# A decoder trunk on one core: other places in SBUF for the tiles

## The chip, the core and the metric

The kernel runs on one core of one Trainium2 chip. The time is device microseconds of that core, as the median of several executions; lower is better. Names used below: PE is TensorE's matmul, PEld its weight load, DVE is VectorE, ACT is ScalarE, POOL is GpSimd, SP is SyncE, whose queue issues nearly all DMAs. SBUF is the on-chip memory, 128 partitions; a tile here has all 128 partitions and a number of bytes in each. "Place" means the byte within the partition at which a tile starts, and "phase" that place modulo a power of two.

## The reference

The reference is a decoder trunk of two layers over 256 tokens of width 2048, in float32. Layer 0 is a recurrent block, layer 1 a sliding-window attention block; each is followed by a SwiGLU FFN of width 5632. Between the layers one K/V is projected.

```python
def swiglu_ffn(x, g, w_in, w_out):
    h = rms_norm(x, g)
    gate, up = jnp.split(h @ w_in, 2, axis=-1)
    return x + (jax.nn.silu(gate) * up) @ w_out

def recurrent_block(x, g, w_in, conv_w, conv_b, w_rg, b_rg, w_ig, b_ig, lam, w_out):
    h = rms_norm(x, g)
    y_branch, x_branch = jnp.split(h @ w_in, 2, axis=-1)
    xb = causal_depthwise_conv(x_branch, conv_w, conv_b)
    hs = rg_lru(xb, w_rg, b_rg, w_ig, b_ig, lam)
    return x + (hs * jax.nn.gelu(y_branch)) @ w_out

def reference(...):
    for layer in range(DEPTH):        # DEPTH = 2, N_REC = 1
        if layer < N_REC:
            x = recurrent_block(x, ...)
        else:
            if layer == N_REC:
                k_band, v_band = shared_kv(x, kv_norm_g, w_kv, k_norm_g)
            x = attn_block(x, ..., k_band, v_band)
        x = swiglu_ffn(x, norm2_g[layer], ffn_w_in[layer], ffn_w_out[layer])
    return x
```

## The kernel before

The activations are held transposed: features in the partitions, the 256 tokens along the free axis. The residual stream is four tiles x0 to x3 of 4 x 256 float32.

All weights are read once, as a stream of tiles of 128 x 1024 float32 (512 KB; 256 rows by 512 columns of a weight matrix). `stream` (line 271) runs over them. For job i it issues the load of tile i+4 on SP's queue (`load`, line 228, into raw[i % 4]), splits tile i+3 (`split`, line 254) and emits the matmuls of tile i. To split means to write each float32 number as the sum of two that the matmul type float32r holds: ScalarE copies raw to hi (line 259), and VectorE writes lo = raw - hi (line 260). The activations are split in the same way into slots of 2 x 256 columns (`split_act`, line 405; `gained`, line 411): the first 256 columns hold the high part, the second 256 the low part. A product then takes three matmuls of 256 moving columns on line 323: weights hi by activation high, hi by low, lo by high. Where two PSUM banks are at hand, the first two are one matmul of 512 columns ("h" in `PARTS`, line 287); `products` (line 289) does this in runs of three. In these the stationary operand is a slice of 128 columns (512 bytes) of hi or lo, and the moving operand is a slot (1024 or 2048 bytes). In the K/V projection (lines 841 to 843) it is the other way round for the values: a slice of hi or lo moves.

The other work (norms, convolution, recurrence, softmax, the activation functions) is cut into small tasks that `run_bg` (line 200) puts between the matmuls, by a count of the time that VectorE and ScalarE are behind. The order of all instructions is fixed when the program is built.

The tiles are made in the constructor (lines 70 to 97) and in `run` (lines 1039 to 1043). Each pool places its tiles one behind the other in the order in which they are made, each rounded up to 32 bytes; the 58 slots get their places when each is first used. The order before is: par, con and cc (parameters and constants), x0 to x3, raw0 to raw3, hi0 to hi3, lo0 to lo3, then the scratch tiles t0 to t3 and h0 to h7 of 256 float32, rstd0 and rstd1 (the per-token scale, 258 float32), acc, sq0 and sq1, then the slots s0 to s57 of 2048 bytes, and in a second pool nm, nt, r2 and rr0 to rr3.

Of the kernel before, what the change touches and what calls it, by code (L numbers as in the profile page):

```python
# [12 lines left out]
F32 = mybir.dt.float32  # L13
F32R = mybir.dt.float32r
# [3 lines left out]
P = 128  # L18
D = 2048
T = 256  # L20
# [20 lines left out]
class Val:  # L41


    def __init__(self, ap=None):
        self.ap = ap
        self.ready = False


class Trunk:
# [18 lines left out]
    def __init__(self, ctx, tc, dram):  # L68
        self.tc, self.nc, self.d = tc, tc.nc, dram
        nc = self.nc  # L70
        const = ctx.enter_context(tc.tile_pool(name="const", bufs=1))
        psum = ctx.enter_context(tc.tile_pool(name="psum", bufs=1, space=bass.MemoryType.PSUM))
        tmp = ctx.enter_context(tc.tile_pool(name="tmp", bufs=1))
        self.tmp = tmp
        self.par = const.tile([P, NPAR], F32, name="par")
        self.con = const.tile([P, NCON], F32, name="con")
        self.cc = const.tile([P, 32], F32, name="cc")
        self.x = [const.tile([P, 4, T], F32, name=f"x{i}") for i in range(4)]
        self.slots = deque(range(58))
        self.spool = const  # L80
        self.held = {}
        self.raw = [const.tile([P, 1024], F32, name=f"raw{i}") for i in range(4)]
        self.hi = [const.tile([P, 1024], F32R, name=f"hi{i}") for i in range(4)]
        self.lo = [const.tile([P, 1024], F32R, name=f"lo{i}") for i in range(4)]
        self.banks = deque(psum.tile([P, 512], F32, name=f"b{i}") for i in range(8))
        self.misc = 0
        self.started = False
        self.xin = 0
        self.other = None
        self.runs = 0  # L90
        self.since = 0
        self.hold = False
        self.tmps = deque(const.tile([P, T], F32, name=f"t{i}") for i in range(4))
        self.halves = deque(const.tile([P, T], F32, name=f"h{i}") for i in range(8))
        self.rstd = [const.tile([P, T + 2], F32, name=f"rstd{i}") for i in range(2)]
        self.acc = const.tile([P, T], F32, name="acc")
        self.sq = deque(const.tile([P, T], F32, name=f"sq{i}") for i in range(2))
        self.jobs = []
        self.bg = deque()
        self.tick = -2 * self.LD  # L100
        self.dve = 0.0
        self.act = 0.0
# [186 lines left out]
    def products(self, todo, st, hi, lo, x2, last, keep=False, paired=False):  # L289
# [7 lines left out]
        while rest:  # L297
            if not ticked and n >= half and not (self.since == 0 and rest[0][2] == "h"):
                self.half_tick()
                ticked = True  # L300
            if self.other is not None:
                self.runs = self.RUNS
            if not keep and self.runs and rest[0][2] != "h":
                left = set(rest)
                run = [(k, f) for k in range(2) for f in range(4) if ps[f][1] and (k, f, "a") in left
                       and (k, f, "b") in left][:3]
                new = ps[rest[0][1]][1] and ps[rest[0][1]][2] not in begun
                due = self.other is not None or self.since % 3 == 1 and self.since > 3
                if len(run) == 3 and (new or due and ps[run[0][1]][2] in begun):
                    self.runs -= 1  # L310
                    rest = [(k, f, "h") for k, f in run] + [q for q in rest if q[:2] not in run or q[2] == "l"]
            k, f, p = rest.pop(0)
            n += 1 + (p == "h")
            self.since = 0 if p == "h" else self.since + 1
            high, c0, c1 = self.PARTS[p]
            w = (hi if high else lo)[:, k * 512 + f * P:k * 512 + f * P + P]
            args = (ps[f][0][:, 0:c1 - c0], w, x2[k][:, c0:c1])
            kw = dict(start=ps[f][2] not in begun, stop=last and all(q[1] != f for q in rest), skip_group_check=paired)
            if self.other is not None and p == "h":
                with self.tc.issue_after(self.other):  # L320
                    self.nc.tensor.matmul(*args, **kw)  # L321
            else:
                self.nc.tensor.matmul(*args, **kw)  # L323
            self.other = None
            begun.add(ps[f][2])
# [710 lines left out]

    def run(self):
        nc, d = self.nc, self.d
        const = self.tmp
        self.nm = const.tile([P, T + 2], F32, name="nm")  # L1040
        self.nt = const.tile([P, T + 2], F32, name="nt")
        self.r2 = const.tile([P, 2], F32, name="r2")
        self.rrs = [const.tile([P, 48], F32, name=f"rr{i}") for i in range(4)]
        self.rv = {i: Val() for i in range(4)}
        self.rstd = {0: self.rstd[0], 1: self.rstd[1], 2: self.rstd[0], 3: self.rstd[1]}
        vals = lambda: [Val() for _ in range(ND)]
        self.xs0, x1, xk, x2, x3 = (vals() for _ in range(5))

        def first():
            for k in range(ND):  # L1050
                while k >= self.xin:
                    yield 1
                self.gained(k, [(C_N1A, self.xs0)])
                yield 2 * (k == 1)
            for k in range(ND):
                yield from self.squares(k)
            yield from self.norm(0, self.NORM0)
            self.decay()
        self.spawn(first())

        self.lru([(C_N2A, x1)], 1)
        self.ffn(0, x1, 1, [(C_KVG, xk)], 2)
        self.kv(xk, 2, [(C_N1B, x2)])
        self.attn(x2, 2, [(C_N2B, x3)], 3)
        self.ffn(1, x3, 3, None, None, out=d["out"])
        self.stream()
# [64 lines left out]
```

## Time and profile before

| What | us |
|---|---|
| median of 3 runs | 1990.03 (1989.65 to 1990.34) |
| span of the profiled execution | 1988.6 |
| PE, first and last matmul of line 268 | start 1.2 to 4.3 |
| DVE busy | 1271.2 |
| ACT busy | 1067.9 |

The span runs from the first to the last instruction of the profiled execution; it is 1.4 us below the median of the runs.

How the views are read: the page's busy line gives, for each engine, the time with at least one instruction in flight. Matmuls are pipelined, so a matmul's duration (its latency) overlaps the next one's; the distance between two starts in the timeline is what a matmul costs in a stream. The timeline joins neighbouring instructions of one group into a row with the first one's start, the row's length and a count; a weight load (PEld) stands beside the matmul before it. The chain that ended last is followed back from the last instruction to whatever released each one.

### The profile page before, as it was taken

Reading aid. Unit: us, or ns where it says so; the run is one execution under the profiler, and the core shown is the slowest. Engines: PE = TensorE matmul, PEld = TensorE weight load, DVE = VectorE, ACT = ScalarE, POOL = GpSimd, SP = SyncE. Lnnn points to the kernel's source line nnn. Section 1 sums busy time; section 2 is a strip of 40 time slices with the busy share of each in tenths; the row PEclk is TensorE's granted clock in tenths of the full one; section 3 lists DMA queues with packets and bytes.
Section 4 is the critical chain, followed back from the end, with each engine's and each line's share of the span. In section 5 each row is a group of like instructions: output and inputs, shape, how many; then the busy total and the mean of one; then the engine's idle time right before and its main releaser. Section 6 shows DMA issues by size and latency. Waiting matters only on the chain.

```text
span 1988.6 us, 40066 instructions
## 1 busy us (share of the span) xinstructions
PE 1982.0 (100%) x16684; PEld 1935.5 (97%) x16684; DVE 1271.2 (64%) x2049; ACT 1067.9 (54%) x1624; POOL 0.2 (0%) x4
## 2 busy tenths in 40 slices
PE   9999999999999999999999999999999999999999
PEld 9999999999999999999999889999999999999999
DVE  8988876556556655545668786755565565554453
ACT  7798655444444444444556775544454454444442
POOL 0000000000000000000000000000000000000000
PEclk9999999999999999999999999999999999999999
DMA  8555655565556555556555435565566656656663
GB/s 279 185 187 182 211 191 192 196 196 191 192 195 196 191 192 196 195 191 194 197 186 167 134 101 163 188 197 195 191 193 196 195 191 194 197 193 203 204 208 128
DMA packets 105302, 376.58 MB, mean 189 GB/s; under 512 B 11808, under 2 KB 14240, under 8 KB 105120
## 3 DMA queue, kind: packets, MB, share of 16 engines
q1 hardware_dynamic: 104832, 373.88, 57.8%
q8 instruction: 130, 2.13, 0.4%
q14 instruction: 52, 0.43, 0.1%
q10 hardware_dynamic: 288, 0.14, 0.0%
HBM read 371.88 MB, written 2.10 MB: 188 GB/s over the span
## 4 chain that ended last, share of the span: by engine, by line
PE 99%; ACT 0%; DVE 0%; DMA 0%; issue 0%; ACTq 0%
PE b L323 94%; PE b L334 2%; PE b L641 1%; PE b L331 1%; PE b L832 1%; ACT s L113 0%; PE b L321 0%; PE b L841 0%; PE b L842 0%; PE b L843 0%; DMA x<-in_x 0%; DVE s L131 0%; DVE lo L260 0%; ACT L113 0%; DVE s L122 0%
## 5 line engine op out<-in xcount | busy, mean ns | idle before, releaser
L323 PE MATMUL b<-s,hi 128*128 128x256 f32 (+1 forms) x10276 | 1431.9, 285 | 0.4 <-ACT s L113 0.4
L323 PEld LDWEIGHTS b<-s,hi 128*128 128x128 f32 x10276 | 1313.4, 188 | 30.4 <-ACT s L113 0.7
L260 DVE TENSOR_TENSOR lo<-raw,hi 128x1024 fp32r<-128x1024 f32 (+1 forms) x705 | 861.4, 1223 | 651.2 <-ACT hi L259 648.1
L259 ACT ACTIVATE hi<-raw 128x1024 fp32r<-128x1024 f32 (+1 forms) x705 | 745.7, 1059 | 817.7 <-PE b L323 756.7
L323 PE MATMUL b<-s,lo 128*128 128x256 f32 x5504 | 831.8, 277 | 0.0
L323 PEld LDWEIGHTS b<-s,lo 128*128 128x128 f32 x5504 | 720.4, 188 | 2.4 <-issue 0.8
L113 ACT ACTIVATE s<-h 128x256 fp32r<-128x256 f32 (+1 forms) x106 | 40.8, 411 | 23.8 <-DVE h L122 23.8
L113 ACT ACTIVATE t<-b 128x256 f32<-128x256 f32 x136 | 49.8, 374 | 2.5 <-PE b L323 0.3
L113 ACT ACTIVATE s<-x,par 128x256 fp32r<-128x256 f32 x80 | 38.6, 499 | 19.3 <-DVE x L122 13.6
L113 ACT ACTIVATE s<-s 128x256 f32<-128x256 f32 (+1 forms) x112 | 39.6, 409 | 5.7 <-DVE s L126 5.5
L113 ACT ACTIVATE h<-h 128x256 f32<-128x256 f32 (+1 forms) x104 | 38.8, 375 | 2.1
L113 ACT ACT_TABLE_LOAD x30 | 38.5, 1283 | 0.5
L126 DVE SCALAR_TENSOR_TENSOR s<-x,par,s 128x256 fp32r<-128x256 f32 x80 | 37.5, 482 | 1.4 <-ACT s L113 0.8
L122 DVE TENSOR_TENSOR h<-b,rstd 128x256 f32<-128x256 f32 x100 | 37.6, 417 | 0.0
L122 DVE TENSOR_TENSOR x<-x,b 128x256 f32<-128x256 f32 x64 | 24.1, 418 | 21.0 <-PE b L323 21.0
L113 ACT ACTIVATE s<-s,h 128x128 f32<-128x128 f32 x64 | 28.3, 443 | 13.3 <-DVE h L131 13.2
L122 DVE TENSOR_TENSOR h<-h,rstd 128x256 f32<-128x256 f32 x94 | 35.4, 419 | 0.0
L122 DVE TENSOR_TENSOR h<-h,h 128x256 f32<-128x256 f32 x88 | 35.0, 420 | 0.4 <-ACT h L113 0.4
L122 DVE TENSOR_TENSOR s<-h,s 128x256 fp32r<-128x256 f32 x88 | 35.2, 420 | 0.1
L122 DVE TENSOR_TENSOR h<-b,t 128x256 f32<-128x256 f32 x92 | 34.6, 417 | 0.0
L122 DVE TENSOR_TENSOR s<-s,s 128x256 fp32r<-128x256 f32 (+1 forms) x80 | 30.9, 422 | 3.5 <-ACT s L113 3.5
L334 PE MATMUL b<-s,s 64*128 64x256 f32 (+3 forms) x292 | 29.0, 302 | 0.1
(99 smaller groups left out, 566.4 us busy)
## 6 DMA issues: line engine op xcount, KB each, us to landing
raw<-in_ffn_in SPq DMA_DIRECT2D x352, 512.0 KB, 3.5
raw<-in_ffn_out SPq DMA_DIRECT2D x176, 512.0 KB, 4.3
raw<-in_lru_in SPq DMA_DIRECT2D x63, 512.0 KB, 3.6
raw<-in_lru_out SPq DMA_DIRECT2D x32, 512.0 KB, 3.7
raw<-in_w_q SPq DMA_DIRECT2D x32, 512.0 KB, 3.3
raw<-in_w_o SPq DMA_DIRECT2D x32, 512.0 KB, 3.3
raw<-in_gate SPq DMA_DIRECT2D x8, 512.0 KB, 3.9
raw<-in_kv SPq DMA_DIRECT2D x8, 512.0 KB, 4.3
```

Of the source, the lines that this page charges most:

```text
L113: self.nc.scalar.activation(out, in_, func, **kw)
L122: self.nc.vector.tensor_tensor(out, a, b, op)
L126: self.nc.vector.scalar_tensor_tensor(out, a, s, b, op0, op1)
L259: self.nc.scalar.activation(hi[:, q], raw[:, q], AF.Copy)
L260: self.nc.vector.tensor_tensor(lo[:, q], raw[:, q], hi[:, q].bitcast(F32), ALU.subtract)
L323: self.nc.tensor.matmul(*args, **kw)
L331: self.other = self.ins(f(*args, **kw))
L334: self.other = self.ins(f(*args, **kw))
L641: nc.tensor.matmul(out[j], (hi if high else lo)[:, c:c + P], x2[kt][:, q:q + T], start=kt == 0 and high > q, stop=kt == 1 and not high)
L832: nc.tensor.matmul(ps[f][:, 0:T], w0, x2[kt][:, q:q + T], start=k0 + kt == 0 and high > q, stop=k0 + kt == ND - 1 and not high)
```

## The change

The change only alters the order in which tiles are made, and adds one tile that nothing uses. After par, con and cc come the small tiles (rstd0, rstd1, nm, nt, r2, rr0 to rr3), then a tile `gap` of 160 float32 (640 bytes), then the scratch tiles t, h, acc and sq, then x, raw, hi and lo; the slots follow as before. The second pool is gone: nm, nt, r2 and rr come from the first.

```diff
-        tmp = ctx.enter_context(tc.tile_pool(name="tmp", bufs=1))
-        self.tmp = tmp
         self.par = const.tile([P, NPAR], F32, name="par")
         self.con = const.tile([P, NCON], F32, name="con")
         self.cc = const.tile([P, 32], F32, name="cc")
+        self.rstd = [const.tile([P, T + 2], F32, name=f"rstd{i}") for i in range(2)]
+        self.nm = const.tile([P, T + 2], F32, name="nm")
+        self.nt = const.tile([P, T + 2], F32, name="nt")
+        self.r2 = const.tile([P, 2], F32, name="r2")
+        self.rrs = [const.tile([P, 48], F32, name=f"rr{i}") for i in range(4)]
+        self.gap = const.tile([P, 160], F32, name="gap")
+        self.tmps = deque(const.tile([P, T], F32, name=f"t{i}") for i in range(4))
+        self.halves = deque(const.tile([P, T], F32, name=f"h{i}") for i in range(8))
+        self.acc = const.tile([P, T], F32, name="acc")
+        self.sq = deque(const.tile([P, T], F32, name=f"sq{i}") for i in range(2))
         self.x = [const.tile([P, 4, T], F32, name=f"x{i}") for i in range(4)]
+        self.raw = [const.tile([P, 1024], F32, name=f"raw{i}") for i in range(4)]
+        self.hi = [const.tile([P, 1024], F32R, name=f"hi{i}") for i in range(4)]
+        self.lo = [const.tile([P, 1024], F32R, name=f"lo{i}") for i in range(4)]
         self.slots = deque(range(58))
...
-        self.raw = [const.tile([P, 1024], F32, name=f"raw{i}") for i in range(4)]
-        self.hi = [const.tile([P, 1024], F32R, name=f"hi{i}") for i in range(4)]
-        self.lo = [const.tile([P, 1024], F32R, name=f"lo{i}") for i in range(4)]
...
     def run(self):
         nc, d = self.nc, self.d
-        const = self.tmp
-        self.nm = const.tile([P, T + 2], F32, name="nm")
...
```

The places that follow, as the built programs have them (bytes within the partition, and the same modulo 2048):

| Tiles | before | after |
|---|---|---|
| x0 | 21984 (1504) | 43008 (0) |
| raw0, hi0, lo0 | 38368, 54752, 71136 (1504 each) | 59392, 75776, 92160 (0 each) |
| t0, t1 | 87520, 88544 (1504, 480) | 27648, 28672 (1024, 0) |
| acc, sq0 | 101920, 102944 (1568, 544) | 39936, 40960 (1024, 0) |
| slots, s0 | 104992 (544) | 108544 (0) |
| rstd0, rstd1 | 99808, 100864 (1504, 512) | 21984, 23040 (1504, 512) |
| par, con | 16512, 17632 (128, 1248) | the same |

More of the change, by code (lines that the diff above doesn't have):

```diff
@@ L92, in __init__ @@
         self.hold = False
[L93 to L97, printed above, removed]
         self.jobs = []
@@ L1038, in run @@
         nc, d = self.nc, self.d
-        const = self.tmp
-        self.nm = const.tile([P, T + 2], F32, name="nm")
-        self.nt = const.tile([P, T + 2], F32, name="nt")
-        self.r2 = const.tile([P, 2], F32, name="r2")
-        self.rrs = [const.tile([P, 48], F32, name=f"rr{i}") for i in range(4)]
         self.rv = {i: Val() for i in range(4)}
```

## Prediction

> **What bounds the kernel now.** I read the page first, then the groups by form, then the timeline of TensorE and of its weight loads. The reader should see in the page that TensorE is never out of work, at the full granted clock, and that the chain that ended last is TensorE alone.
>
> ```profile
> span 1988.6 us, 40066 instructions
> PE 1982.0 (100%) x16684; PEld 1935.5 (97%) x16684; DVE 1271.2 (64%) x2049; ACT 1067.9 (54%) x1624; POOL 0.2 (0%) x4
> PEclk9999999999999999999999999999999999999999
> PE 99%; ACT 0%; DVE 0%; DMA 0%; issue 0%; ACTq 0%
> ```
>
> So only two things can move the end: the spacing of the matmuls, or a new wait in front of TensorE. The groups by form say which matmuls there are (count, then busy us and mean ns of one; the mean is a latency, not a spacing):
>
> ```profile
> L323 PE MATMUL b<-s,hi 128*128 128x256 f32 x9570 | 1291.3, 277 | 0.4 <-ACT s L113 0.4
> L323 PE MATMUL b<-s,lo 128*128 128x256 f32 x5504 | 831.8, 277 | 0.0
> L323 PE MATMUL b<-s,hi 128*128 128x512 f32 x706 | 201.6, 393 | 0.0
> ```
>
> That is 9570 + 5504 = 15,074 matmuls of 256 columns and 706 of 512 on line 323. The spacing is read from starts in the timeline (start us, busy us, engine, group, count):
>
> ```profile
> 1976.12 0.98 PEld L323 LDWEIGHTS b<-s,lo 128*128 128x128 f32 x8
> 1976.23 1.07 PE L323 MATMUL b<-s,lo 128*128 128x256 f32 x8
> ...
> 1977.13 1.98 PE L323 MATMUL b<-s,hi 128*128 128x256 f32 x16
> ...
> 1978.95 1.07 PE L323 MATMUL b<-s,lo 128*128 128x256 f32 x8
> ...
> 1979.85 1.98 PE L323 MATMUL b<-s,hi 128*128 128x256 f32 x16
> ...
> 1981.67 1.07 PE L323 MATMUL b<-s,lo 128*128 128x256 f32 x8
> ...
> 1982.57 0.39 PE L323 MATMUL b<-s,hi 128*128 128x256 f32 x2
> ```
>
> From 1976.23 to 1982.57 there are 8+16+8+16+8 = 56 matmuls in 6.34 us, 113.2 ns each. The load of the first one's weights starts at 1976.12, 110 ns ahead of it, so almost the whole spacing is one weight load. Loads with nearly no matmul behind them (the moving operand has one column) come at 42.20, 42.31, 42.42 and 42.53, 0.33 us for three, 110 ns each:
>
> ```profile
> 42.20 0.30 PEld L334 LDWEIGHTS b<-con,acc 128*128 128x128 f32 x2
> 42.31 0.30 PEld L334 LDWEIGHTS b<-con,acc 128*128 128x128 f32 x2
> 42.42 0.19 PEld L334 LDWEIGHTS b<-con,acc 128*128 128x128 f32 x1
> 42.53 0.19 PEld L321 LDWEIGHTS b<-s,hi 128*128 128x128 f32 x1
> ```
>
> A 256-column matmul is therefore paced by its weight load. A 512-column one is not: in a run of three the starts lie 0.23 us apart.
>
> ```profile
> 1223.37 0.62 PE L323 MATMUL b<-s,hi 128*128 128x512 f32 x2
> 1223.60 0.62 PE L323 MATMUL b<-s,hi 128*128 128x512 f32 x2
> 1223.83 0.62 PE L323 MATMUL b<-s,hi 128*128 128x512 f32 x3
> ```
>
> There is a second spacing for 256 columns. Here 8+16+8 matmuls, from 157.69 to 161.46, take 3.77 us, 117.8 ns each:
>
> ```profile
> 157.69 1.10 PE L323 MATMUL b<-s,lo 128*128 128x256 f32 x8
> 158.64 2.05 PE L323 MATMUL b<-s,hi 128*128 128x256 f32 x16
> 160.52 1.10 PE L323 MATMUL b<-s,lo 128*128 128x256 f32 x8
> 161.46 2.05 PE L323 MATMUL b<-s,hi 128*128 128x256 f32 x16
> ```
>
> **The change part by part.** It removes no instruction and adds none. In the two built programs the five engines have the same instructions in the same order with the same waits, and SP's queue has the same DMA issues; nothing is moved past a queue. What moves is the place of the tiles inside a partition. Before, x, raw, hi and lo start 1504 bytes past a multiple of 2048, the split activations 544 past it, t and h alternately at 1504 and 480. Every one of these lies 32 past a multiple of 64. After, x (43008 = 21 x 2048), raw, hi, lo and the split activations start at multiples of 2048, the scratch tiles at multiples of 1024. The gap tile is never read or written. So each access has to be priced by kind.
>
> *256-column matmuls and their weight loads.* Does their spacing know the address? All starts on line 323 share the remainder 32 by 64, so the trace has no aligned case. It has other phases, however. On lines 841 to 843 the moving operand is a slice of the weights (480 past 2048) and the stationary one an activation; on line 832 it is the other way round (moving at 544 or 1568):
>
> ```profile
> 1018.46 0.28 PE L842 MATMUL b<-lo,s 128*128 128x256 f32 x1
> ...
> 1019.37 0.39 PE L832 MATMUL b<-s,hi 128*128 128x256 f32 x2
> ...
> 1020.73 0.28 PE L841 MATMUL b<-hi,s 128*128 128x256 f32 x1
> ...
> 1021.91 0.28 PE L842 MATMUL b<-lo,s 128*128 128x256 f32 x1
> ```
>
> Eight matmuls up to 1019.37 take 0.91 us, 114 ns each; the twelve of line 832 up to 1020.73 take 1.36 us, 113 ns each; and ten more up to 1021.91 take 1.18 us, 118 ns each. Both spacings occur with the same phases, and the fast one occurs with either. I take 0 for this term. Its bounds: down to the 110 ns of a load alone, 15,074 x 3.2 ns = 48 us less (an estimate); up to 117.8 ns throughout, 15,074 x 4.6 ns = 69 us more (an estimate, a little high, since some run so already).
>
> *512-column matmuls.* [...] Lower bound: two spacings of a load alone, 220 ns, so 706 x 10 ns = 7 us less. Upper bound: two of the slow spacing, 236 ns, 4 us more. I take 0, as the activations' halves at 544 and 1568 serve the same spacing.
>
> [...]
>
> *VectorE and ScalarE.* The per-token scale has two tiles: rstd0 starts 32 past a multiple of 64, rstd1 on one. Most of the first group below are the FFNs' and read rstd1; the second is the recurrent block's and reads rstd0 (min/median/max ns):
>
> ```profile
> L122 DVE TENSOR_TENSOR h<-h,rstd x94: 416/419/433, 154.9 to 1746.6; 128x256 f32<-128x256 f32 x94
> L122 DVE TENSOR_TENSOR s<-s,rstd x8: 417/420/426, 50.5 to 76.2; 128x256 f32<-128x256 f32 x8
> ```
>
> 419 against 420 ns: the operand's place does not show. A gain here would be worth nothing, since TensorE waits for neither engine. A loss would be covered by their idle time, except where VectorE is nearly full:
>
> ```profile
> 0.00:20.00 20.00, 18.41 (x110) 17.39 (x111) 13.74 (x38) 15.21 (x28) 0.20 (x4) 1.00 0.89 328
> 20.00:160.00 140.00, 140.00 (x1193) 138.27 (x1192) 129.34 (x252) 111.58 (x188) 0.00 (x0) 1.00 0.62 199
> ```
>
> (Columns: window, length, busy us and count of PE, PEld, DVE, ACT, POOL, granted clock, DMA share, GB/s.) VectorE is busy for 129.34 of 140 us there, so a VectorE 8% slower would fill that stage; 10% would cost 142.3 - 140 = 2 us. I take 0.
>
> *DMA.* The share is 0.62 there. A load lands 3.5 us after its issue, and the split that uses it (line 259) waits for TensorE to free its hi tile, not for a DMA:
>
> ```profile
> L259 ACT ACTIVATE hi<-raw 128x1024 fp32r<-128x1024 f32 x703 | 744.5, 1060 | 816.8 <-PE b L323 756.7 <-issue 41.9 <-PE b L843 5.9
> raw<-in_ffn_in SPq DMA_DIRECT2D x352, 512.0 KB, 3.5
> ```
>
> So faster or slower writes stay hidden behind 756.7 us of such waits. Only the start is exposed, in the chain of waits:
>
> ```profile
> 1.16 3.34 DMA x<-in_x
> 5.16 36.78 PE b L323 x274
> ```
>
> The first projection matmul at 5.16 us stands behind a 3.34 us transfer. A tenth of that is 0.3 us either way, the bound of this term; I take 0.
>
> **Sum.** 0 + 0 + 0 + 0 on the profiled span of 1988.6 us. The runs' median is 1990.03 us, 1.4 us above the span, and that is the same for both programs. Forecast: 1990.0 us, no change.
>
> **The rivals.**
>
> *Faster: the two reads of TensorE cost less at aligned places.* For it: 113.2 ns is above the 110 ns of a load alone, and 230 ns is above twice that, while TensorE waits for nothing, so something in the operand supply costs 3 ns in 256 columns and 10 ns in 512. All starts share one remainder by 64, so alignment can be that something. Against it: the loads alone have the same remainder and need only 110 ns, and other phases change nothing. If only the 512s gain, 1990.0 - 7 = 1983 us. With half of the rest, 1990.0 - 7 - 24 = 1959 us; with all of it, 1990.0 - 55 = 1935 us. [...]
>
> *Slower: the slow spacing spreads.* Before, the weights' start and the moving operand's start differ by 1504 - 544 = 960 bytes, 448 by 512; after, by 0, so both of TensorE's reads begin at the same phase. If such reads get in each other's way, the state with 117.8 ns is entered more often. For it: that state exists, lasts over whole stages and shows no other engine as its cause. Against it: it occurs at both phases of the rows from 1018 to 1022. A quarter of the 256s costs 15,074 x 4.6 / 4 = 17 us, so 2007 us; all of them 69 us, 2059 us. It decides from 4 us on, some 900 matmuls.
>
> *The change does not do what it says.* A tile placed elsewhere by the allocator would leave the old remainders. The built program has the addresses given above, so this holds only for effects: it is the forecast.
>
> **How the numbers follow.** About 0.2%, 4 us, is what a measurement of this kernel can tell from no change. No change 0.42, its own range 1986 to 1994. Faster 0.33: 0.12 for the 512s alone near 1983, 0.12 for up to half of the rest, 0.09 beyond that. Slower 0.25: 0.16 for up to a quarter and a bit, 0.09 beyond. Together 8 in 10 need 1958 to 2018, which leaves out the 0.09 and 0.09 at the ends. The predicted time is that of the likeliest case.
>
> **What would show it.** Right: the spacing in the last 56 matmuls stays 113 ns, runs of 512 columns stay at 230 ns, the stretch from 157 to 161 us still shows 118, and the split of line 259 keeps its mean of 1060 ns. The faster rival shows as a 256 spacing near 110, or a 512 spacing near 220, everywhere at once. The slower one shows as 118 in stretches that have 113 now. A first projection matmul well away from 5.16 us would make the DMA term wrong; a wait of TensorE for VectorE between 20 and 160 us would make the cover wrong.

## The result, and the profile after

| | before | after |
|---|---|---|
| median of 4 runs, us | 1990.12 (1989.65 to 1990.34) | 2086.48 (2086.18 to 2086.78) |
| profiled span, us | 1988.6 | 2084.4 |

The changed kernel is slower: the ratio is 1.0484, with a 95% interval of 1.0471 to 1.0497. The spans differ by 95.8 us. Lines of the changed file stand three further down: 323 is now 326, 259 is 262.

The page of the kernel after, in the lines that answer to those shown of before:

```profile
span 2084.4 us, 40066 instructions
PE 2076.7 (100%) x16684; PEld 2029.1 (97%) x16684; DVE 1272.6 (61%) x2049; ACT 1065.3 (51%) x1624; POOL 0.2 (0%) x4
...
PEclk9999999999999999999999999999999999999999
...
PE 99%; ACT 0%; DMA 0%; DVE 0%; SPq 0%; issue 0%
```

The instruction counts are the same, the granted clock is the same, and TensorE is as fully in use as before. VectorE and ScalarE are busy for as long as before. TensorE is idle for 2084.4 - 2076.7 = 7.7 us, where it was idle for 6.6. So it has no new wait that counts; each matmul takes more time. The timeline near the end of the kernel after (start us, busy us, engine, group, count):

```profile
2072.48 2.08 PE L326 MATMUL b<-s,hi 128*128 128x256 f32 x16
2074.40 1.12 PE L326 MATMUL b<-s,lo 128*128 128x256 f32 x8
2075.36 2.08 PE L326 MATMUL b<-s,hi 128*128 128x256 f32 x16
2077.28 1.12 PE L326 MATMUL b<-s,lo 128*128 128x256 f32 x8
2078.24 0.40 PE L326 MATMUL b<-s,hi 128*128 128x256 f32 x2
```

From 2072.48 to 2078.24 there are 48 matmuls in 5.76 us, 120.0 ns each, where there were 113.2. This is not a feature of the end. The windows of a long, even stretch of both kernels say the same; the columns are the window, its length, busy us and count for PE, PEld, DVE, ACT and POOL, the clock, the DMA share and GB/s. Before:

```profile
400.00:1000.00 600.00, 600.00 (x5104) 592.26 (x5103) 348.93 (x454) 284.53 (x370) 0.00 (x0) 1.00 0.60 194
```

After:

```profile
400.00:1000.00 600.00, 600.00 (x4831) 591.82 (x4830) 326.06 (x424) 263.27 (x342) 0.00 (x0) 1.00 0.56 184
```

In 600 us TensorE gets through 4831 matmuls instead of 5104, 5.3% fewer, with a busy row that looks the same. The count, not the busy time, shows the loss. Everything else only follows: fewer matmuls, so fewer splits and fewer loads.

The other terms of the prediction, in the groups and the timeline of after. The weight loads with nearly no matmul behind them:

```profile
43.41 0.30 PEld L337 LDWEIGHTS b<-con,acc 128*128 128x128 f32 x2
43.51 0.30 PEld L337 LDWEIGHTS b<-con,acc 128*128 128x128 f32 x2
43.63 0.19 PEld L337 LDWEIGHTS b<-con,acc 128*128 128x128 f32 x1
43.74 0.19 PEld L324 LDWEIGHTS b<-s,hi 128*128 128x128 f32 x1
```

Three of them still take 0.33 us, 110 ns each. A load alone has not become slower. The runs of 512 columns:

```profile
1323.93 0.63 PE L326 MATMUL b<-s,hi 128*128 128x512 f32 x2
1324.16 0.62 PE L326 MATMUL b<-s,hi 128*128 128x512 f32 x2
1324.40 0.51 PE L326 MATMUL b<-s,hi 128*128 128x512 f32 x2
```

They start 0.23 to 0.24 us apart, hardly more than before. The split, VectorE's products with the two scale tiles (min/median/max ns), and the first matmuls of the projection:

```profile
L262 ACT ACTIVATE hi<-raw 128x1024 fp32r<-128x1024 f32 x703 | 743.2, 1058 | 923.7 <-PE b L326 839.8 <-issue 50.9 <-ACT h L116 18.2
```

```profile
L125 DVE TENSOR_TENSOR h<-h,rstd x94: 406/415/420, 159.3 to 1828.5; 128x256 f32<-128x256 f32 x94
L125 DVE TENSOR_TENSOR s<-s,rstd x8: 412/416/426, 51.8 to 77.8; 128x256 f32<-128x256 f32 x8
```

```profile
5.26 1.49 PE L326 MATMUL b<-s,hi 128*128 128x256 f32 x6 [0.68 <-ACT s L116]
```

The split takes 1058 ns where it took 1060, the products 4 ns less, and the first matmul comes 0.1 us later. None of this carries 96 us.

A finer number is used below, "the mean spacing": over the trace's starts of all 256-column matmuls of the projections' line (15,015 to 15,038 of them in each run), the mean distance to the next matmul's start, gaps outside 100 to 130 ns left out. It is 113.6 ns before and 119.8 after. Then 15,074 x 6.2 ns = 93 us, and the 706 of 512 columns went from 229.5 to 232.5 ns (in the same way, gaps outside 200 to 260 ns left out), 706 x 3.0 = 2 us. Together 95 us of the 95.8.

### The profile page after: what moved, and what is told of

Its sections match the earlier page's. It is cut to its first block, busy times and chain, and to the rows that moved or that the text cites. A ratio compares the mean times of both kernels' runs of the same rounds, so it can differ in the third digit from the quotient of the medians.

```text
span 2084.4 us, 40066 instructions
## 1 busy us (share of the span) xinstructions
PE 2076.7 (100%) x16684; PEld 2029.1 (97%) x16684; DVE 1272.6 (61%) x2049; ACT 1065.3 (51%) x1624; POOL 0.2 (0%) x4
## 4 chain that ended last, share of the span: by engine, by line
PE 99%; ACT 0%; DMA 0%; DVE 0%; SPq 0%; issue 0%
PE b L326 94%; PE b L337 2%; PE b L644 1%; PE b L334 1%; PE b L835 1%; DMA raw<-in_lru_in 0%; ACT s L116 0%; PE b L324 0%; PE b L845 0%; PE b L844 0%; PE b L846 0%; DVE s L134 0%; ACT L116 0%; DVE lo L263 0%; ACT hi L262 0%
## 5 line engine op out<-in xcount | busy, mean ns | idle before, releaser
L326 PE MATMUL b<-s,hi 128*128 128x256 f32 (+1 forms) x10276 | 1495.0, 291 | 1.7 <-ACT hi L262 1.0
L326 PEld LDWEIGHTS b<-s,hi 128*128 128x128 f32 x10276 | 1368.8, 191 | 33.1 <-ACT hi L262 1.4
L262 ACT ACTIVATE hi<-raw 128x1024 fp32r<-128x1024 f32 (+1 forms) x705 | 744.5, 1057 | 926.0 <-PE b L326 839.8
L326 PE MATMUL b<-s,lo 128*128 128x256 f32 x5504 | 865.3, 283 | 0.0
L326 PEld LDWEIGHTS b<-s,lo 128*128 128x128 f32 x5504 | 751.0, 192 | 2.3 <-issue 0.8
L116 ACT ACTIVATE h<-h 128x256 f32<-128x256 f32 (+1 forms) x104 | 34.3, 370 | 0.0
```

What stands on the lines that cost most here:

```text
L116: self.nc.scalar.activation(out, in_, func, **kw)
L262: self.nc.scalar.activation(hi[:, q], raw[:, q], AF.Copy)
```

## The experiments

Each was executed once, beside the kernel before on the same chip, which took 1989.4 to 1990.4 us there. In the theories, "distance" is the start of the activations' slots minus the start of hi and lo, modulo 256; slices are multiples of 512 bytes and halves of 1024, so one number holds for all matmuls of the projections. Before it is 544 - 1504 = -960, which is 64; after it is 0.

### Is it alignment, the distance, or the other engines?

**All tiles 32 bytes further.**

```diff
-        self.gap = const.tile([P, 160], F32, name="gap")
+        self.gap = const.tile([P, 168], F32, name="gap")
```

> The kernel after with 32 more bytes of gap: t, h, acc, sq, x, raw, hi, lo and the slots all start 32 past where they start after, so no operand of TensorE starts on a multiple of 64, but weights and activations still start at the same phase (32 modulo 512 for both). Theory R (TensorE's two reads get in each other's way when they begin at the same phase; only the difference counts): 120 ns between 256-column matmuls as after, about 2086 us. Rival A (a read that starts on a multiple of 64 or more is slower; the place itself counts): 113 ns as before, about 1990 us. Rival T (VectorE, ScalarE or DMA accesses at the same phase as TensorE's, all tiles together): 120 ns, about 2086 us.

Measured: 2086.53 us. None of the tiles behind the gap starts on a multiple of 64 any more, and nothing was gained. Rival A is out.

**Only the slots 64 bytes further.**

```diff
         self.lo = [const.tile([P, 1024], F32R, name=f"lo{i}") for i in range(4)]
+        self.pad = const.tile([P, 16], F32, name="pad")
```

> The kernel after with 64 bytes between lo and the slots: only the activations' slots move, to 64 past a multiple of 2048; weights, x, raw and scratch stay at multiples of 1024 and 2048. The slots then lie 64 past the weights by 512, as before. Theory R: 113 ns, about 1990 us. Rival A (multiples of 64 are slower): 120 ns, about 2086 us. Rival T: the slots alone leave the common phase; raw, hi, lo and x, which carry most of the other engines' traffic, still share it, so most of the loss stays, over 2050 us.

Measured: 1990.77 us, the whole loss gone with 64 bytes. The window of this run has before's count:

```profile
400.00:1000.00 600.00, 600.00 (x5104) 592.23 (x5103) 348.81 (x454) 284.48 (x371) 0.00 (x0) 1.00 0.59 194
```

x, raw, hi, lo and scratch share their phase as they do after, so rival T is out too.

**The kernel before, with its slots brought to the weights' phase.**

```diff
         self.sq = deque(const.tile([P, T], F32, name=f"sq{i}") for i in range(2))
+        self.pad = const.tile([P, 112], F32, name="pad")
```

> The kernel before with 448 bytes between sq and the slots: the slots start 992 past a multiple of 2048, 480 modulo 512 like the weights; nothing lies on a multiple of 64. Theory R: the loss appears without any alignment, 120 ns, about 2086 us. Rival A: nothing starts on a multiple of 64, 113 ns, about 1990 us. Rival T: raw, hi, lo, x and scratch stand to each other as before, about 1990 us.

Measured: 2088.10 us. The loss of the change appears in the kernel before without any of its alignment:

```profile
400.00:1000.00 600.00, 600.00 (x4831) 591.82 (x4830) 327.46 (x427) 263.38 (x342) 0.00 (x0) 1.00 0.56 184
```

**The weights moved instead of the slots.**

```diff
+        self.pad = const.tile([P, 48], F32, name="pad")
         self.hi = [const.tile([P, 1024], F32R, name=f"hi{i}") for i in range(4)]
         self.lo = [const.tile([P, 1024], F32R, name=f"lo{i}") for i in range(4)]
+        self.pad2 = const.tile([P, 16], F32, name="pad2")
```

> The kernel after with 192 bytes between raw and hi and 64 between lo and the slots: hi and lo start 192 past a multiple of 256, the slots on one. The activations thus lie 64 past the weights modulo 256, but now by moving the weights; x, raw, t, h, acc and sq stay where they are after. Theory R (only the distance from the weights to the activations counts): 113 ns, about 1990 us. Rival M (the phase of the moving operand itself counts, as in the runs where only the slots moved; here it is a multiple of 256 as after): 120 ns, about 2085 us.

Measured: 1990.80 us, mean spacing 113.6 ns. The slots start on a multiple of 256 as after, and it costs nothing: the distance decides, not the place of either operand. x, raw and the scratch tiles still stand at the slots' phase here, as they do after, so accesses to them do not carry the loss either. What the other engines still share with the weights' place is the writing of hi and lo, and the trace of after answers for that: in the 1587 gaps behind a hi matmul of line 326 during which neither VectorE nor ScalarE has an instruction in flight, the mean is 120.0 ns; in 913 such gaps of before it is 113.4, and 114.0 in the 1873 in which one instruction of each is in flight from end to end. The price is paid without these engines.

### hi at the cheap distance, lo at the dear one

```diff
+        self.pad = const.tile([P, 48], F32, name="pad")
         self.hi = [const.tile([P, 1024], F32R, name=f"hi{i}") for i in range(4)]
+        self.pad2 = const.tile([P, 16], F32, name="pad2")
         self.lo = [const.tile([P, 1024], F32R, name=f"lo{i}") for i in range(4)]
```

> The kernel after with 192 bytes between raw and hi and 64 between hi and lo: seen from hi the activations are 64 ahead modulo 256 (the cheap distance), seen from lo they are at the same phase (the dear one). Theory R-next (a matmul's reading is disturbed by the load of the next matmul's weights, which runs beside it): in a block of hi matmuls 113 ns, in a block of lo matmuls 120 ns, and the step lies one matmul ahead of the block's border (the last hi of a block, with a lo load beside it, already takes 120). With 5504 of the 256-column matmuls in lo, 5504 x 6.7 = 37 us, about 2027 us. Rival R-all (one bad pair sets the pace for both): about 2085 us. Rival: a cheap hi carries over to lo, about 1990 us.

Measured: 2026.92 us, the time expected of R-next. The timeline of this run changes its pace from block to block (line 328 is the projections' matmul):

```profile
501.88 1.07 PE L328 MATMUL b<-s,hi 128*128 128x256 f32 x8
502.79 1.12 PE L328 MATMUL b<-s,lo 128*128 128x256 f32 x8
503.75 2.44 PE L328 MATMUL b<-s,hi 128*128 128x256 f32 x17
```

Eight hi matmuls take 0.91 us, eight lo matmuls 0.96 us, 114 and 120 ns. Over the whole run hi has a mean spacing of 113.8 ns and lo of 120.0. Both rivals are out: a bad pair costs its 6 to 7 ns and leaves the other pairs nearly alone. What set R-next apart did not come either: the step does not lie a matmul early. From the starts, a hi matmul followed by lo takes 115.2 ns on average and a lo followed by hi 120.8. The recorded spacing goes with a matmul's own weights, not with those loaded beside its recorded start. So it is shown that each pair of weight slice and moving activations costs by its distance; by what mechanism is not.

### The map of distances

The diff is always that of the slots above with another length of `pad`: 64 floats for 256 bytes, 32 for 128, and so on.

> The kernel after with 256 bytes between lo and the slots: the slots start half of 512 away from the weights' phase. Theory R: not 120 ns if the period is 512 or more, between 110 and 118 ns, 1940 to 2060 us; still 120 ns if the pattern repeats every 256 bytes or less. Rival A: 120 ns, about 2086 us. Rival T: over 2050 us.

> The kernel after with the slots 128 bytes past the weights' phase. Theory R128 (what counts is the distance modulo 128, so 0, 128 and 256 are alike): 120 ns, about 2086 us. Rival R256 (the pattern repeats only every 256 bytes, and 128 is the farthest from a clash): 113 ns or less, 1990 us or below.

> The kernel after with the slots 192 bytes past the weights' phase, 64 modulo 128. Theory R128: the same as 64, 113 ns, about 1990 us. Rival R256: no reason to equal 64; it mirrors it at best, and lies between 113 and 120 ns, 1990 to 2086 us.

> The kernel after with the slots 32 bytes past the weights' phase. Theory W64 (each read takes 64 bytes at a time from one of two alternating halves of SBUF, and only reads of the same half clash): 32 overlaps half of the clash, so the spacing lies between 113 and 120 ns, about 2040 us. Rival L (only exactly equal phases clash): 113 ns or less, 1990 us or below. Rival S (a step: anything under 64 counts as the same): 120 ns, 2086 us.

> The kernel after with the slots 96 bytes past the weights' phase, which is 32 before the next multiple of 128. Theory W64: between 113 and 120 ns, about 2040 us, like 32. Rival L: 113 ns or less, 1990 us or below. Rival S: like 64, 113 ns, about 1990 us.

> The kernel after with the slots 160 bytes past the weights' phase. The runs at 0, 32, 64, 96, 128, 192 and 256 gave 2086, 2045, 1991, 2089, 2069, 2054 and 2086 us, so 256 bytes repeat and the curve is not smooth. If a clash is a matter of nearness to 0 modulo 256: between 128 and 192, about 2060 us. If there is a cheap place every 128 bytes less 32: it could be as cheap as 64, about 1990 us.

> The kernel after with the slots 224 bytes past the weights' phase, 32 short of a full turn. If nearness to 0 modulo 256 is the matter: between 192 (2054) and 256 (2086), about 2070 us. If the curve has a second cheap place: below 2000 us, and below 1990 us it would beat both kernels.

> The kernel after with the slots 320 bytes past the weights' phase, 64 modulo 256. If the pattern repeats every 256 bytes, as the equal times at 0 and 256 suggest: 113 ns, about 1991 us, as at 64. If 0 and 256 were alike for another reason (both are multiples of 128 and 256, and 512 is the turn): between 113 and 120 ns, over 2000 us.

For distances between multiples of 32, hi and lo of the kernel before were made longer by 256 bytes and used from a later byte on, here for 48 (the others use 60:1084, 2:1026 and 62:1086, for 80, 56 and 72):

```diff
-        self.hi = [const.tile([P, 1024], F32R, name=f"hi{i}") for i in range(4)]
-        self.lo = [const.tile([P, 1024], F32R, name=f"lo{i}") for i in range(4)]
+        self.hi = [const.tile([P, 1088], F32R, name=f"hi{i}")[:, 4:1028] for i in range(4)]
+        self.lo = [const.tile([P, 1088], F32R, name=f"lo{i}")[:, 4:1028] for i in range(4)]
```

> The kernel before with each hi and lo tile 256 bytes longer and used from its 16th byte on: the phase of the weights moves by 16, so the activations lie 48 past the weights modulo 256 instead of 64; nothing else changes its phase. The map in steps of 32 has 117.1 ns at 32, 113.6 at 64 and 120.0 at 96. If the cheap place is a hole as narrow as one step: between 113.6 and 117.1, about 115 ns, 2015 us. If 64 only sits on the edge of a wider hole: 113 ns or less, and with 110 ns (a load alone) 1940 us, which would beat both kernels.

> The same with the weights used from byte 240 on, 16 short of a full turn: the activations lie 80 past the weights modulo 256. If the cheap place is a hole as narrow as one step: between 113.6 and 120.0, about 117 ns, 2040 us. If the hole reaches up to 96: 113 ns or less, 1940 to 1990 us.

> The kernel before with longer hi and lo tiles used from their 8th byte on: the activations lie 56 past the weights modulo 256. The runs at 48 and 80 gave 2037 and 2059 us against 1990 at 64. If the curve falls evenly to 64 from both sides: between 1990 and 2037, about 2010 us. If the bottom lies between 48 and 64: below 1990 us, at best 1940 us with 110 ns.

> The same with the weights used from byte 248 on: the activations lie 72 past the weights modulo 256. If the curve falls evenly to 64: between 1990 and 2059, about 2020 us. If the bottom lies between 64 and 80: below 1990 us, at best 1940 us.

Measured, with the mean spacing of the 256-column matmuls:

| distance modulo 256 | us | mean spacing, ns |
|---|---|---|
| 0 (after; slots at 0) | 2086.48 | 119.8 |
| 0 (slots 256 past the weights) | 2085.90 | 119.8 |
| 32 | 2044.67 | 117.1 |
| 48 | 2037.22 | 116.7 |
| 56 | 2059.65 | 118.1 |
| 64 (before) | 1990.12 | 113.6 |
| 64 (after + 64; after + 320) | 1990.77; 1990.53 | 113.6; 113.6 |
| 72 | 2057.11 | 117.9 |
| 80 | 2059.29 | 118.1 |
| 96 | 2089.18 | 120.0 |
| 128 | 2069.20 | 118.7 |
| 160 | 2050.63 | 117.5 |
| 192 | 2053.90 | 117.7 |
| 224 | 2064.50 | 118.4 |

What follows. Where it was tried, the pattern repeats after 256 bytes (0 and 256, 64 and 320). It is not a matter of nearness: 96 is dearer than 0, though it lies 32 from the cheapest place, and 160 does not lie between 128 and 192 but slightly under both. R128 fell, since 0 and 128 differ by 17 us; R256 fell at 128, where it had 1990 us or below; and so did the smooth picture of W64: 32 came at 2045 us as it had it, but 96 is not like 32. The halves of SBUF in W64 were the author's guess and were not shown. L and S, the two rivals at 32, fell as well. A second cheap place, for which the expectations for 160 and 224 allowed, is at neither. The cheap place at 64 is a narrow hole, as one expectation for 48 and 80 had it. It is dear even 8 bytes to either side: the run at 56 lies above the ranges of both its expectations, and the one at 72 at the upper end of the first (at 56 and 72 the weights start on a multiple of 8 that is not one of 16, and what that alone costs was not measured; at 48 and 80 they start on multiples of 16, and the spacing is 116.7 and 118.1 ns). A distance below 113 ns was not found, so no layout tried beats the kernel before. Why the curve has this shape is open. Multiples of 32 are mapped in full; of the finer distances only these four were tried.

## Why the prediction was wrong

**What bounds the kernel.** Right: the end is set by the spacing of the matmuls, before and after, and TensorE gained no wait that matters. That the weight load alone paces a 256-column matmul was not shown, though: a 512-column one takes 229.5 ns on average, and half of that, 114.8, is nearer to the spacing of 113.2 than the 110 ns of a load. Loads alone still take 110 ns after the change, and the spacing is 120.

**No instruction moves.** Right, and it is the reason that the whole loss can be read from one number.

**The 256-column matmuls: the step that failed.** The prediction took 0 for this term, from the rows between 1018 and 1022 us, where "both spacings occur with the same phases". The rows were read rightly; the step from them to "no effect" failed. It compared the places of single operands, and these do not matter, as the run with everything 32 bytes further (2086.53 us) and the run with moved weights (1990.80 us) show. What matters is the distance, and those rows hold two of them only: 64 on line 832, as on line 323, and, from the stationary to the moving operand, 480 - 544 = -64, which is 192, on lines 841 to 843. Two blocks of twelve that lie just ahead of the prediction's rows start here:

```profile
1016.58 0.40 PE L832 MATMUL b<-s,hi 128*128 128x256 f32 x2
...
1018.00 0.28 PE L841 MATMUL b<-hi,s 128*128 128x256 f32 x1
```

The block at 64 from 1016.58 to 1018.00 takes 118 ns for each, the block at 192 from there to 1019.37 takes 114; the next at 64 takes 113, and the next at 192 takes 118. So each of the two distances has both spacings there. After, at distance 0, both kinds of block take 1.44 us, 120 ns for each:

```profile
1065.09 0.40 PE L835 MATMUL b<-s,hi 128*128 128x256 f32 x2
...
1066.53 0.28 PE L844 MATMUL b<-hi,s 128*128 128x256 f32 x1
...
1067.97 0.40 PE L835 MATMUL b<-s,hi 128*128 128x256 f32 x2
```

That two distances behave alike was taken to mean that every distance does, and the one to which the change goes, 0, was not among them. In the trace of before only the matmuls of line 268 read both operands from the same place, and they mostly lie 213 to 214 ns apart in both kernels, so they say nothing of a stream at 113. Even 64 and 192 are not alike in the projections, where they differ in which spacing rules: at 64, 13,756 of 15,018 gaps are 113 or 114 ns and some 900 are 117 to 119; at 192, 14,624 of 15,033 are 117 to 119 and some 370 are 113 or 114. What puts a stretch into one spacing or the other was not tried.

**The bound of that term.** The upper bound, 117.8 ns for every matmul, was the dearest spacing seen before, and was taken for the dearest there is. The measured spacing is 119.8, 6.2 ns more than before over 15,074 matmuls: +93 us where the bound had +69. Every other distance measured has 116.7 to 120.0, so by the spacings of the map a layout that did not keep 64 was in for a loss of some 47 to 96 us. The rows of before that the prediction used could not tell that, since they hold 64 and 192 alone.

**512 columns.** The term was 0 with a bound of +4 us; it is +2 us. Right within its bound.

**VectorE, ScalarE, DMA.** Right: 1058 against 1060 ns, 415 against 419 ns, and a first matmul at 5.26 us against 5.16, inside the 0.3 us allowed. The aligned transfers are worth nothing, as the wait is for TensorE's hi tiles: 839.8 of the 923.7 us that ScalarE is idle ahead of the split.

**The faster rival.** Fell. Its argument was that 113 ns is above the 110 ns of a load alone and that alignment could be the rest. With everything off the multiples of 64 or on them, the time is the same at the same distance (2086.53 and 2086.48 us), and no distance went below 113.6. What the 3 ns are is open.

**The slower rival.** It came nearest: it named the difference of the two starts, and that the change takes it to 0. Its mechanism, two reads of TensorE in each other's way, was not shown: the runs give a time for each distance, not its cause. Nor is beginning at the same phase what makes a distance dear, since 96 (120.0 ns) is dearer than 0 (119.8). Its price was off, too. It expected the state of 117.8 ns to be entered more often and gave the far end 2059 us and a chance of 0.09; in fact the distance 0 has a spacing of its own, 120 ns, in every stage at once: the means of the windows from 20 to 160, 310 to 1014, 1060 to 1300 and 1300 to 1700 us lie between 119.5 and 119.9. The state of 117.8 is not that one. At the distance 64 it is the exception, as in the stretch from 157 to 190 us, with an interruption at its start (gaps of 212 and 214 ns) and a run of 512 columns at its end; at 192 its spacing is the rule. Its cause was not tried.

## What to carry to other kernels

Where TensorE is the bound and streams float32r as here, a weight load before each matmul of 256 columns, look at the place of the stationary tiles and that of the moving tiles together: their distance modulo 256 bytes was worth up to 5% here (1990.12 us at 64, 2089.18 at 96), and any edit that adds, drops or reorders a tile between them can change it. Compare the time between two starts in the timeline, or the count of matmuls in a window, not busy time. And a trace that shows no dependence has only shown it for the cases that it contains: list those cases first, in the variable that could matter.

## What the runs showed of the hardware

That the pace of TensorE goes with the distance between its two SBUF operands was not expected. At distance 0 a 256-column matmul takes 119.8 ns on average, at 64 it takes 113.6, at the other distances measured 116.7 to 120.0. Distances 0 and 64 were each tried at several places and gave the same mean, and the price of 0 is paid while VectorE and ScalarE have nothing in flight. Against distance 64, weights and activations at the dearest distance, 96, cost 6.4 ns more per matmul on average. By what mechanism was not shown.

Second, the spacing at a dear distance can be uneven in a regular way. The same window of the run at 32 holds 4935 matmuls, between the 5104 of distance 64 and the 4831 of distance 0:

```profile
400.00:1000.00 600.00, 600.00 (x4935) 591.45 (x4934) 336.38 (x439) 274.26 (x357) 0.00 (x0) 1.00 0.57 188
```

Its single gaps from 500 to 504 us run 113 or 114, 116, 117 or 118, 120 over and over. At distance 0 they do not: 13,651 of the 15,035 of after are 120 ns. So the price of a distance can be a mean over a short cycle, and need not be one fixed delay.
